# The tiled products of scores and values between the two products of the inverses' blocks

## The chip, the cores and the metric

One Trainium2 chip, one core. The metric is the device time of one execution in microseconds, the median over several runs. The kernel is written in Bass and Tile: Tile orders the instructions of each engine by priority and sets the semaphores; where the kernel asks for it, the order of TensorE's instructions is that of the program text.

## The reference

A trunk of one layer: 512 positions, width 2048, in two groups of channels, the first of 16 heads of 64 channels with a generalized delta rule, the second a multi-scale pooling. What matters here is the first:

```
def step(S, inp):
    r_t, w_t, k_t, v_t, kk_t, a_t = inp
    sa = jnp.einsum('bhvk,bhk->bhv', S, -kk_t)
    S = (S * w_t[:, :, None, :]
         + sa[..., None] * (kk_t * a_t)[:, :, None, :]
         + v_t[..., None] * k_t[:, :, None, :])
    y_t = jnp.einsum('bhvk,bhk->bhv', S, r_t)
    return S, y_t
```

Ahead of it stand an RMS norm, the projection `h @ w_in` to 6272 columns and a token shift; behind it a norm per head, a gate, the projections `w_out` and `w_pg`, an embedding term and a last RMS norm.

## The kernel before

**The stages.** First the input is normed, transposed and split into two parts (`hhi`, `hlo`); a dense product in this kernel is three matmuls of 128x128 on 512 columns (`mm3`, L164: high by high, high by low, low by high). Then, from about 55 to 715 us, eight pairs of heads `j` are worked off, two heads and 128 channels each, the 512 positions in 8 chunks of 64. The last stage is the two large projections with `w_out` and `w_pg`.

**The stream.** The recurrence over the chunks is a chain of small steps on TensorE, ScalarE and VectorE. So that TensorE does not idle meanwhile, the projections of the next pairs (`zr`, `zk`, `zv`, `zg`) and of the pooling group (`zb`, with `pp`) run between its steps: `stream()` (L461) is a generator that yields after every three dense matmuls, and `pump(n)` (L492) takes some n matmuls from it. It carries over what it took too much (`debt`). The weights of the stream come by DMA on SP's queue and are split by a cast on ScalarE (L132, `whi`) and a subtraction on VectorE (L133, `wlo`), two chunks ahead of their use.

**The order on TensorE.** From L345 on, `pin` is set: `mm` and `tr` (L156, L160) call `keep_in_program_order`, so TensorE runs its instructions in the order in which the code writes them. The other engines are ordered by Tile's priorities. `tc.high_priority(offset=HP)`, with HP = 1000, puts the instructions of its block ahead of others that could go as well.

**One pair.** `prepare(j)` scales keys and receptances; `scores(j)` (L608) makes the scores within chunks (`mt`, 64x64 blocks) and sends their 32x32 corners by DMA to a layout in which `invert(j)` (L650) inverts the unit triangular matrices on VectorE; the inverses' diagonal blocks come back by DMA into `x1`. `gather(j)` (L678) then finishes what the recurrence needs, and `recur(j)` (L756) runs it.

**`gather`, step by step, on TensorE** (every small product is in fp32, which TensorE runs as two matmul instructions; 16 products are 32 instructions):

- `decay_and_rate` for the next pair (`pu`, `pa`), transposes of the values (`pv`, L688) and of the keys (`pbk`, L699). ScalarE copies them to `uv` (L690, L691) and `bkn` (L700).
- `pump(H4)`: 8 dense matmuls, in effect 9.
- `pmv` (L704): 16 products of scores and values on 64x64 tiles. ScalarE copies the result into `zsp[0]` (L712) and `mv` (L713).
- `norm_key(j + 1)`: two dense matmuls `pss`, read by VectorE (L568).
- `pump(H5)`, the four transposes `pyt` of the pair before, `pump(HX)`.
- `pq` (L738): 16 products of 32x32 blocks, the scores' corner times the inverse's first block, which VectorE has transposed (`y1`, L734). ScalarE copies the result to `q2t` in two halves (L745; the profile calls the tile `q`).
- `pump(H1)`: 6 dense matmuls.
- `px` (L747): 16 products of 32x32 blocks, `q2t` times the inverse's second block. ScalarE copies the result into the corner of `x1` (L752; the profile calls the tile `x`).
- `pump(H1)`: 6 dense matmuls; then the recurrence begins with `pu`, which reads `x1` and `zsp[0]` (L793). `mv` is first read one step later, in the sum into `zs` (L787).

`pmv`, `pss`, `pyt`, `pq` and `px`, and ahead of them `pu`, `pa` and `pbk`, are tiles of the PSUM pool `psM` under one tag with three buffers; a fourth tile waits until the first one has been read.

Of the kernel before, what the change touches and what calls it, by code (L numbers as in the profile page):

```python
# [9 lines left out]
F32 = mybir.dt.float32  # L10
# [5 lines left out]
P = 128  # L16
# [7 lines left out]
C = 64  # L24
# [10 lines left out]
def trunk_kernel(ctx: ExitStack, tc: tile.TileContext, x, p, norm_g, w_in, mu, w0, w_up, a0, a_up,  # L35
                 k_k, k_a, r_k, ln_w, ln_b, w_pool, pool_scale, w_out, w_ple, w_pg, b_pg, final_g, out):
    nc = tc.nc
    PSUM = bass.MemoryType.PSUM
    x, p, w_in, w_out, w_ple, w_pg = x[0], p[0, 0], w_in[0], w_out[0], w_ple[0], w_pg[0]
# [8 lines left out]
    psM = s2.enter_context(tc.tile_pool(name="psM", bufs=3, space=PSUM))  # L48
# [107 lines left out]
    def mm(*a, **k):  # L156
        i = nc.tensor.matmul(*a, **k)  # L157
        return tc.keep_in_program_order(i) if pin[0] else i

    def tr(*a):  # L160
        i = nc.tensor.transpose(*a)
        return tc.keep_in_program_order(i) if pin[0] else i
# [178 lines left out]
    rw = s2a.enter_context(tc.tile_pool(name="rw", bufs=1))  # L341
# [18 lines left out]
    zsp = [rw.tile([P, P], F32, name=f"zs{i}") for i in range(2)]  # L360
# [131 lines left out]
    def pump(n):  # L492
        debt[0] += n
        while debt[0] > 0:
            c = next(big, None)
            if c is None:
                debt[0] = 0
                return
            debt[0] -= c
# [17 lines left out]
    H1, H2, H3, H4, H5, HE = 6, 12, 20, 8, 13, 40  # L517

    def decay_and_rate(j):

        (ur, us), (ar_, as_) = wab.pop(j)
        for raw, st, z_, lo, hi in ((ur, us, uaz[0], slice(64, 128), slice(0, 64)),
                                    (ar_, as_, uaz[1], slice(0, 64), slice(64, 128))):
            nc.scalar.copy(st, raw)
            nc.scalar.copy(z_[hi, :], raw[hi, :])
            nc.vector.tensor_tensor(st[lo, :], raw[lo, :], st[lo, :].bitcast(F32), ALU.subtract)

        ps = psM.tile([P, T], F32, name=f"pu{j}", tag="m")
        mm(ps, us, uhh, start=True, stop=False)
        mm(ps, uaz[0], lal, start=False, stop=True)  # L530
        sig = rw.tile([P, T], F32, name=f"sig{j}", tag="t", bufs=4)
        nc.scalar.activation(sig, ps, AF.Tanh, scale=0.5, bias=dp(81, j))
        nc.vector.tensor_scalar(sig, sig, 0.5, 0.5, ALU.mult, ALU.add)
        nc.vector.tensor_tensor_scan(sig, seg, sig, 0.0, ALU.mult, ALU.add)
        pw = rw.tile([P, NCH, C + 1], F32, name=f"pw{j}", tag="pw", bufs=2)
        ipw = rw.tile([P, NCH, C], F32, name=f"ipw{j}", tag="ipw")
        nc.gpsimd.memset(pw[:, :, 0:1], 1.0)
        sig3 = sig.rearrange("p (c t) -> p c t", t=C)
        nc.scalar.activation(pw[:, :, 1:C + 1], sig3, AF.Exp, scale=-KAPPA)
        nc.scalar.activation(ipw, sig3, AF.Exp, scale=KAPPA)  # L540


        ps = psM.tile([P, T], F32, name=f"pa{j}", tag="m")
        mm(ps, as_, ahh, start=True, stop=False)
        mm(ps, uaz[1], lal, start=False, stop=True)
        tha = rw.tile([P, T], F32, name=f"tha{j}", tag="tha")
        nc.scalar.activation(tha, ps, AF.Tanh, scale=0.5, bias=dp(25, j))
        pws[j] = (pw, ipw, tha)
# [5 lines left out]
    def prepare_key(j):  # L554
        k_ = need("k", j)
        kk = rw.tile([P, T], F32, name=f"kk{j}", tag="kk")
        nc.scalar.activation(kk, k_, AF.Square, scale=pc("k_k", j))
        kqh = rw.tile([P, T], F32R, name=f"kqh{j}", tag="t", bufs=4)
        kql = rw.tile([P, T], F32R, name=f"kql{j}", tag="t", bufs=4)
        split(kqh, kql, kk)  # L560
        kks[j] = (kk, kqh, kql)

    def norm_key(j):
        kk, kqh, kql = kks[j]
        ps = psM.tile([P, T], F32, name=f"pss{j}", tag="m")
        mm(ps, blk, kqh, start=True, stop=False)
        mm(ps, blk, kql, start=False, stop=True)
        late[0] = nc.vector.tensor_scalar(kk, ps, 1e-24, None, ALU.max)  # L568

    def scale_key(j):  # L570
        k_, kk = need("k", j), kks[j][0]
        nc.vector.reciprocal(kk, kk)
        nc.vector.scalar_tensor_tensor(kk, k_, pc("k_k", j), kk, ALU.mult, ALU.mult)
        kks[j] = kk
# [103 lines left out]
    def gather(j):  # L678
        d = st_[j]
        bk, v_, mt = d.pop("bk"), d.pop("v_"), d["mt"]  # L680
        if j + 1 < NJ:
            prepare_key(j + 1)
            decay_and_rate(j + 1)

        uv = rw.tile([P, NCH, P], F32, name=f"uv{j}", tag="uv")
        ps = psY.tile([P, T], F32, name=f"pv{j}", tag="y")
        for tt in range(NT):
            tr(ps[:, tt * P:(tt + 1) * P], v_[:, tt * P:(tt + 1) * P], ident)  # L688
        pv = ps.rearrange("p (t c) -> p t c", c=P)
        nc.scalar.copy(uv[0:64, 0::2, :], pv[0:64])  # L690
        nc.scalar.copy(uv[64:128, 1::2, :], pv[64:128])  # L691


        bkn = rw.tile([P, NCH, P], F32, name=f"bkn{j}", tag="bkn")
        for hf in range(2):
            ps = psM.tile([P, T], F32, name=f"pbk{j}_{hf}", tag="m")
            for i in range(4):
                ch = 4 * hf + i
                tr(ps[:, i * P:(i + 1) * P], bk[:, ch // 2, 2 * (ch % 2):2 * (ch % 2) + 2, :], ident)  # L699
            nc.scalar.copy(bkn[:, 4 * hf:4 * hf + 4, :], ps.rearrange("p (c n) -> p c n", n=P))  # L700

        pump(H4)

        ps = psM.tile([P, 8, C], F32, name=f"pmv{j}", tag="m")  # L704
        for u in range(8):
            for par in range(2):
                pb, kb = 64 * (1 - par), 64 * par
                h = u % 2
                mm(ps[pb:pb + 64, u, :], mt[kb:kb + 64, par, u, 1 - par, :],
                   uv[kb:kb + 64, 2 * (u // 2) + par, 64 * h:64 * h + 64], start=True, stop=True)  # L710
        mv = rw.tile([P, 4, P], F32, name=f"mv{j}", tag="mv")
        nc.scalar.copy(zsp[0][64:128, :].rearrange("p (h t) -> p h t", h=2), ps[64:128, 0:2, :])  # L712
        nc.scalar.copy(mv.rearrange("p q (h t) -> p (q h) t", h=2), ps)  # L713

        d.update(uv=uv, bkn=bkn, mv=mv)
        if j + 1 < NJ:
            norm_key(j + 1)
        pump(H5)
        if pending:
            pending.pop()()  # L720
        pump(HX)

        x1 = d["x1"]

        def units(fn):
            for u in range(8):
                for par in range(2):
                    fn(u, par, 64 * (1 - par))

        y1 = rw.tile([P, 8, 32], F32, name=f"y1{j}", tag="tm")  # L730

        with tc.issue_after(late[0].ins):
            for pb in (0, 64):
                yt = nc.vector.transpose(y1[pb:pb + 32], x1[pb:pb + 32, :, 0:32])  # L734
        if j + 1 < NJ:
            with tc.issue_after(yt.ins):
                scale_key(j + 1)
        ps3 = psM.tile([P, 8, 32], F32, name=f"pq2{j}", tag="m")  # L738
        units(lambda u, par, pb: mm(ps3[pb + 32:pb + 64, u, :],
                                                  mt[pb:pb + 32, par, u, 1 - par, 32:64],  # L740
                                                  y1[pb:pb + 32, u, :], start=True, stop=True,
                                                  tile_position=(pb, pb + 32)))
        q2t = rw.tile([P, 8, 32], F32, name=f"q2{j}", tag="xw")
        for pb in (0, 64):
            nc.scalar.copy(q2t[pb + 32:pb + 64], ps3[pb + 32:pb + 64])  # L745
        pump(H1)
        ps4 = psM.tile([P, 8, 32], F32, name=f"px2{j}", tag="m")  # L747
        units(lambda u, par, pb: mm(ps4[pb:pb + 32, u, :], q2t[pb + 32:pb + 64, u, :],
                                                  x1[pb + 32:pb + 64, u, 32:64], start=True, stop=True,
                                                  tile_position=(pb + 32, pb)))  # L750
        for pb in (0, 64):
            nc.scalar.copy(x1[pb:pb + 32, :, 32:64], ps4[pb:pb + 32])  # L752
        pump(H1)


    def recur(j, work, between):  # L756
# [115 lines left out]
    HP = 1000  # L872
# [11 lines left out]
    for _ in invert(0):  # L884
        pass
    pump(HT)
    gather(0)
    for j in range(NJ):
        def between():
# [291 lines left out]
```

## Time and profile before

| what | value |
|---|---|
| time, median of 3 runs | 1099.41 us (1097.35, 1099.41, 1099.85) |
| span of the profiled execution | 1095.9 us |
| median of the runs less that span | 3.5 us |
| stretch from 100 to 715 us: TensorE, VectorE, ScalarE busy | 611.5, 471.1, 262.7 of 615.0 us |

The span goes from the first to the last instruction of one profiled execution; the time of a run also holds what lies around it. The time of the profiled execution itself, apart from its span, is not listed, so the median of the runs stands beside it. A row of a timeline gives the start, the duration, the engine, the line, the operation, the tile written and the tiles read, the size of the part of the array that is used (rows\*columns), and how often; L157 is the line of the helper `mm`, so TensorE's rows are told apart by their tiles. The duration of a matmul covers its whole way through the array: the next one starts well before it ends, so starts are what to compare.

### The profile page before, as it was taken

The numbers are of one execution on the slowest core, as the hardware profiler recorded it, in microseconds if no ns is written. First come the engines' busy times: TensorE is split into PE (matmuls) and PEld (weight loads), VectorE is DVE, ScalarE is ACT, GpSimd is POOL, SyncE is SP. The second block draws the span as 40 slices with busy tenths as digits, with TensorE's granted clock in tenths as the row PEclk, the third lists the DMA queues.
The fourth block names the chain that finished last, engine by engine and source line by source line (L and its number), as shares of the span: only waits on it lengthen the run. The fifth ranks groups of instructions, "written<-read, shape, count | busy, mean of one in ns | idle before, by whom it ended". The sixth has DMA issues, their size and how long they took to land.

```text
span 1095.9 us, 17196 instructions
## 1 busy us (share of the span) xinstructions
PE 1070.8 (98%) x6060; PEld 877.6 (80%) x6060; DVE 708.2 (65%) x1835; ACT 448.3 (41%) x917; POOL 76.9 (7%) x180
## 2 busy tenths in 40 slices
PE   5999999999999999999999999999999999999996
PEld 4888878887788888788878788888888888888885
DVE  6687867878688679678886956454433424445366
ACT  7633535345335335353343344543222222233337
POOL 2100110110110110100101101000000000000000
PEclk9999999999999999999999999999999999999999
DMA  7433433332423333333334242775534438455534
GB/s 233 116 96 97 111 92 84 96 100 73 120 82 105 104 92 89 96 82 93 91 94 119 79 138 93 232 233 169 172 124 136 167 99 244 137 189 137 181 106 154
DMA packets 178486, 138.56 MB, mean 126 GB/s; under 512 B 34678, under 2 KB 139743, under 8 KB 178399
## 3 DMA queue, kind: packets, MB, share of 16 engines
q1 hardware_dynamic: 157694, 103.89, 32.1%
q10 hardware_dynamic: 20704, 33.56, 9.8%
q8 instruction: 48, 0.79, 0.3%
q14 instruction: 40, 0.32, 0.1%
HBM read 118.02 MB, written 18.87 MB: 125 GB/s over the span
## 4 chain that ended last, share of the span: by engine, by line
PE 86%; DVE 5%; DMA 4%; ACT 3%; issue 1%; SPq 0%; ACTq 0%; DVEq 0%
PE acc_o L157 16%; PE zb L157 14%; PE acc_g L157 14%; PE zv L157 8%; PE zk L157 7%; PE zg L157 7%; PE zr L157 7%; PE py L157 2%; PE pple L157 2%; PE pm L157 1%; PE pu L157 1%; DMA n<-nd 1%; PE pp L157 1%; DMA raw_g<-in_w_pg_dram 1%; PE ps L157 1%
## 5 line engine op out<-in xcount | busy, mean ns | idle before, releaser
L133 DVE TENSOR_TENSOR wlo_g<-raw_g,whi_g 128x512 fp32r<-128x512 f32 x84 | 57.0, 685 | 79.6 <-ACT whi_g L132 76.5
L157 PE MATMUL zb<-hhi,whi_b 128*128 128x512 f32 x256 | 107.0, 418 | 0.0
L133 DVE TENSOR_TENSOR wlo_o<-raw_o,whi_o 128x512 fp32r<-128x512 f32 x64 | 43.9, 690 | 91.4 <-ACT whi_o L132 91.4
L157 PE MATMUL zb<-hhi,wlo_b 128*128 128x512 f32 x256 | 100.5, 393 | 0.0
L157 PE MATMUL acc_o<-whi_o,ylo 128*128 128x512 f32 x256 | 100.2, 391 | 0.0
L157 PE MATMUL acc_o<-whi_o,yhi 128*128 128x512 f32 x256 | 99.9, 390 | 0.0
L157 PE MATMUL zb<-hlo,whi_b 128*128 128x512 f32 x256 | 99.9, 390 | 0.0
L157 PE MATMUL acc_o<-wlo_o,yhi 128*128 128x512 f32 x256 | 99.8, 390 | 0.0
L132 ACT CAST whi_g<-raw_g 128x512 fp32r<-128x512 f32 x84 | 51.9, 620 | 102.7 <-PE acc_g L157 55.4
L157 PE MATMUL acc_g<-whi_g,x2hi 128*128 128x512 f32 x208 | 81.3, 391 | 0.0
L157 PE MATMUL acc_g<-wlo_g,x2hi 128*128 128x512 f32 x208 | 80.9, 389 | 0.0
L157 PE MATMUL acc_g<-whi_g,x2lo 128*128 128x512 f32 x208 | 80.7, 389 | 0.0
L132 ACT CAST whi_o<-raw_o 128x512 fp32r<-128x512 f32 x64 | 39.9, 623 | 97.0 <-PE acc_o L157 96.7
L816 POOL TENSOR_SCALAR s0p<-sbd,pw 64x64 f32<-64x64 f32 x96 | 56.6, 589 | 322.8 <-DVE sbd L809 255.0
L132 ACT CAST whi_b<-raw_b 128x512 fp32r<-128x512 f32 x64 | 39.7, 621 | 86.5 <-PE zv L157 35.4
L133 DVE TENSOR_TENSOR wlo_b<-raw_b,whi_b 128x512 fp32r<-128x512 f32 x64 | 43.8, 685 | 34.2 <-ACT whi_b L132 32.9
L157 PEld LDWEIGHTS zb<-hhi,wlo_b 128*128 128x128 f32 x256 | 48.0, 188 | 11.1
L661 DVE TENSOR_TENSOR xw<-xw,tm 128x60 f32<-128x60 f32 (+24 forms) x248 | 52.1, 210 | 6.8
L157 PEld LDWEIGHTS acc_o<-wlo_o,yhi 128*128 128x128 f32 x256 | 48.1, 188 | 10.3 <-DVE wlo_o L133 0.4
L157 PEld LDWEIGHTS acc_o<-whi_o,yhi 128*128 128x128 f32 x256 | 48.1, 188 | 9.7
L157 PEld LDWEIGHTS acc_o<-whi_o,ylo 128*128 128x128 f32 x256 | 48.1, 188 | 9.8
L157 PEld LDWEIGHTS zb<-hhi,whi_b 128*128 128x128 f32 x256 | 48.2, 188 | 8.5
(285 smaller groups left out, 2550.0 us busy)
## 6 DMA issues: line engine op xcount, KB each, us to landing
raw_b<-in_w_in_dram SPq DMA_DIRECT2D x64, 256.0 KB
raw_o<-in_w_out_dram SPq DMA_DIRECT2D x64, 256.0 KB
raw_g<-in_w_pg_dram SPq DMA_DIRECT2D x64, 256.0 KB
raw_k<-in_w_in_dram SPq DMA_DIRECT2D x32, 256.0 KB
raw_r<-in_w_in_dram SPq DMA_DIRECT2D x32, 256.0 KB
raw_v<-in_w_in_dram SPq DMA_DIRECT2D x32, 256.0 KB
raw_g<-in_w_in_dram SPq DMA_DIRECT2D x32, 256.0 KB
n<-nd SPq DMA_DIRECT2D x16, 256.0 KB
```

What stands on the lines that cost most here:

```text
L132: nc.scalar.copy(hi, raw)
L133: nc.vector.tensor_tensor(lo, raw, hi.bitcast(F32), ALU.subtract)
L157: i = nc.tensor.matmul(*a, **k)
L661: nc.vector.tensor_tensor(xw[:, 0:n_, s + 1:32], xw[:, 0:n_, s + 1:32], tm[:, 0:n_, 0:w_], ALU.add)
L816: nc.gpsimd.tensor_scalar(s0p[hc, :], nxt[hc, hc], pcn[hc], None, ALU.mult)
```

## The change

The 16 products of scores and values (`pmv`, now written to `psv`, the same tile name in the profile) leave their place ahead of `norm_key` and stand between `pq` and `px`. The portion of 6 dense matmuls that stood between `pq` and `px` joins the portion behind `px`: 12 dense matmuls there. The copies into `zsp[0]` and `mv` come behind the copies into `x1`. The copies into `q2t` are given high priority. The order of the 16 products (by `u`, then `par`) and their operands stay as they were.

```
-        ps = psM.tile([P, 8, C], F32, name=f"pmv{j}", tag="m")
-        for u in range(8):
-            for par in range(2):
-                pb, kb = 64 * (1 - par), 64 * par
-                h = u % 2
-                mm(ps[pb:pb + 64, u, :], mt[kb:kb + 64, par, u, 1 - par, :],
-                   uv[kb:kb + 64, 2 * (u // 2) + par, 64 * h:64 * h + 64], start=True, stop=True)
-        mv = rw.tile([P, 4, P], F32, name=f"mv{j}", tag="mv")
-        nc.scalar.copy(zsp[0][64:128, :].rearrange("p (h t) -> p h t", h=2), ps[64:128, 0:2, :])
-        nc.scalar.copy(mv.rearrange("p q (h t) -> p (q h) t", h=2), ps)
-
-        d.update(uv=uv, bkn=bkn, mv=mv)
+        d.update(uv=uv, bkn=bkn)
         if j + 1 < NJ:
             norm_key(j + 1)
         pump(H5)
...
         q2t = rw.tile([P, 8, 32], F32, name=f"q2{j}", tag="xw")
-        for pb in (0, 64):
-            nc.scalar.copy(q2t[pb + 32:pb + 64], ps3[pb + 32:pb + 64])
-        pump(H1)
+        with tc.high_priority(offset=HP):
+            for pb in (0, 64):
+                nc.scalar.copy(q2t[pb + 32:pb + 64], ps3[pb + 32:pb + 64])
+        psv = psM.tile([P, 8, C], F32, name=f"pmv{j}", tag="m")
+        units(lambda u, par, pb: mm(psv[pb:pb + 64, u, :], mt[64 - pb:128 - pb, par, u, 1 - par, :],
+                                    uv[64 - pb:128 - pb, 2 * (u // 2) + par, 64 * (u % 2):64 * (u % 2) + 64],
+                                    start=True, stop=True))
         ps4 = psM.tile([P, 8, 32], F32, name=f"px2{j}", tag="m")
...
         for pb in (0, 64):
             nc.scalar.copy(x1[pb:pb + 32, :, 32:64], ps4[pb:pb + 32])
-        pump(H1)
+        mv = rw.tile([P, 4, P], F32, name=f"mv{j}", tag="mv")
+        nc.scalar.copy(zsp[0][64:128, :].rearrange("p (h t) -> p h t", h=2), psv[64:128, 0:2, :])
+        nc.scalar.copy(mv.rearrange("p q (h t) -> p (q h) t", h=2), psv)
+        d["mv"] = mv
+        pump(2 * H1)
```

## The prediction, made before the changed kernel was run

> **What bounds the kernel now.** I read the page first, then the table of who waited for whom, then the timeline of TensorE at the places that the change touches.
>
> ```profile
> span 1095.9 us, 17196 instructions
> PE 1070.8 (98%) x6060; PEld 877.6 (80%) x6060; DVE 708.2 (65%) x1835; ACT 448.3 (41%) x917; POOL 76.9 (7%) x180
> ...
> PE 86%; DVE 5%; DMA 4%; ACT 3%; issue 1%; SPq 0%; ACTq 0%; DVEq 0%
> ```
>
> TensorE is busy 98% of the span, and 86% of the chain that ended last lies on it. "Busy" is modelled from the ends of pipelined matmuls, so I looked for real waits:
>
> ```profile
> PE py L157 <- DVE sbd L809: 1.6, 4, 0.9
> PE pss L157 <- ACT bkn L700: 0.9, 2, 0.5
> ```
>
> Within the eight head pairs TensorE hardly waits for another engine; these are the two largest such waits, with the total, the count and the longest. One, `pss` for ScalarE's `bkn` copy, stands right behind the products that move. Everything else that can be won here is how TensorE's own instructions follow each other. The timeline of gather 0, with the start and the duration of each:
>
> ```profile
> 113.61 0.39 PE L157 MATMUL zv<-hhi,whi_v 128*128 128x512 f32 x1
> 113.84 0.39 PE L157 MATMUL zv<-hlo,whi_v 128*128 128x512 f32 x1
> 114.06 0.39 PE L157 MATMUL zv<-hhi,wlo_v 128*128 128x512 f32 x1
> 114.38 1.15 PE L157 MATMUL pmv<-uv,mt 64*64 64x64 f32 x32
> 115.46 0.50 PE L157 MATMUL pss<-kqh,blk 128*128 128x512 f32 x1
> 115.80 0.39 PE L157 MATMUL pss<-kql,blk 128*128 128x512 f32 x1
> ...
> 121.94 0.39 PE L157 MATMUL zb<-hhi,wlo_b 128*128 128x512 f32 x1
> 122.26 0.69 PE L157 MATMUL pq<-y,mt 32*32 32x32 f32 x32
> 122.89 0.50 PE L157 MATMUL zb<-hhi,whi_b 128*128 128x512 f32 x1
> 123.22 0.40 PE L157 MATMUL zb<-hlo,whi_b 128*128 128x512 f32 x1
> ...
> 124.15 0.39 PE L157 MATMUL zb<-hhi,wlo_b 128*128 128x512 f32 x1
> 124.47 0.69 PE L157 MATMUL px<-x,q 32*32 32x32 f32 x32
> 125.09 0.50 PE L157 MATMUL zb<-hhi,whi_b 128*128 128x512 f32 x1
> 125.43 0.40 PE L157 MATMUL zb<-hlo,whi_b 128*128 128x512 f32 x1
> ```
>
> Dense matmuls start 0.23 apart (113.61, 113.84, 114.06). A visit to small tiles breaks that pace three times: the first small product starts 0.32 after the last dense one, not 0.23; the first dense one starts 0.13 to 0.15 after the last small one; and the second dense one 0.33 or 0.34 after the first. I cost a visit from the last dense start to the second dense start behind it, less two paces (0.46): `pmv` 115.80 - 114.06 - 0.46 = 1.28 us, `pq` 123.22 - 121.94 - 0.46 = 0.82, `px` 125.43 - 124.15 - 0.46 = 0.82. That is 2.92 us per gather. The last of the eight gathers shows the same `pq` visit (648.67 + 0.34 - 647.73 = 1.28 again):
>
> ```profile
> 647.73 0.39 PE L157 MATMUL zb<-hhi,wlo_b 128*128 128x512 f32 x1
> 648.05 0.69 PE L157 MATMUL pq<-y,mt 32*32 32x32 f32 x32
> 648.67 0.50 PE L157 MATMUL zb<-hhi,whi_b 128*128 128x512 f32 x1
> 649.01 0.40 PE L157 MATMUL zb<-hlo,whi_b 128*128 128x512 f32 x1
> ```
>
> The group rows over all eight give what one small product takes, to find the start of the last one:
>
> ```profile
> L157 PE MATMUL pmv<-uv,mt x256: 218/218/267, 114.4 to 641.1; 64*64 64x64 f32 x128
> L157 PE MATMUL pq<-y,mt x256: 191/191/212, 122.3 to 648.5; 32*32 32x32 f32 x128
> ```
>
> So from the first start to the last, 32 products take 0.69 - 0.19 = 0.50 us on 32x32 tiles and 1.15 - 0.22 = 0.93 on 64x64; the wait from the last small start to the next dense one is 122.89 - 122.76 = 0.13 behind `pq` and 115.46 - 115.31 = 0.15 behind `pmv`.
>
> **Term 1: three visits become one.** No product is added or removed: the same 96 small products run, and the same dense ones (the two portions of 6 become one of 12, the next weights stand in the same order). Two entries and two exits to dense work go per gather; two changes of tile size come in, 32x32 to 64x64 and back. No row of this trace has such a change. Nearest are the entries and exits themselves. I take for each what the array leaves empty before the next tile shape may start, 0.13 behind 32x32 and 0.15 behind 64x64. One visit is then 0.32 + 0.50 + 0.13 + 0.93 + 0.15 + 0.50 + 0.13 + 0.33 - 0.46 = 2.53 us, against 2.92: 0.39 saved, eight times, 3.1 us. Bounds: if an inner change costs as much as going out to dense work and back, nothing is saved (0); if it costs only the pace of the small products (0.50/31 = 0.02 and 0.93/31 = 0.03), `px` would follow the last `pq` by 0.02 + 0.93 + 0.03 = 0.98 us instead of 1.21, and then the copy below sets it. The 0.32 in front of `pq` and the 0.13 behind it are the rows that decide for the middle.
>
> [...]
>
> **Term 2: the copy of `q`.** It loses its cover. `px` needs both halves of `q`, which ScalarE copies from `pq`. So far six dense matmuls ran in that time; now only `pmv` does.
>
> ```profile
> 123.05 0.74 ACT L745 COPY q<-pq 32x256 f32<-32x256 f32 x2 [1.74 <-issue]
> 123.81 0.62 ACT L132 CAST whi_g<-raw_g 128x512 fp32r<-128x512 f32 x1
> ```
>
> ```profile
>   PE pq L157: 9.9, 7
> ```
>
> The copies start 0.29 after the last `pq` (122.76) and end 1.03 after it. The row from the view of `q`'s tile counts why ScalarE stood idle before them: in 7 of 8 gathers it was waiting for `pq`, so nothing was ahead. The handover to TensorE is in these rows: `bkn` is two copies of 0.59, the first done at 189.27 + 0.59 = 189.86, and `pss` starts at 189.90, some 0.05 later.
>
> ```profile
> 189.27 1.07 ACT L700 COPY bkn<-pbk 128x512 f32<-128x512 f32 x2
> ...
> 189.90 0.50 PE L157 MATMUL pss<-kqh,blk 128*128 128x512 f32 x1 [0.45 <-ACT bkn L700]
> ```
>
> ```profile
> L700 ACT COPY bkn<-pbk x16: 566/588/597, 114.8 to 639.3; 128x512 f32<-128x512 f32 x16
> ```
>
> So `px` may start 1.03 + 0.05 = 1.08 us after the last `pq`, and by TensorE it would at 0.13 + 0.93 + 0.15 = 1.21. Hidden, with 0.13 to spare. The new high priority puts these copies ahead of other ready work, but not ahead of a cast already running. ScalarE is busy 41%, a cast runs 0.62, so an unlucky start adds up to 0.62 - 0.13; if busy 4 times in 10 with any rest of the cast equally likely, 0.4 x 0.49 x 0.49 / (2 x 0.62) = 0.08 per gather, 0.6 in all. Seven idle arrivals of eight speak for half of that: +0.3 us. If the inner changes were free, the floor of 1.08 would hold, so term 1 would win 0.13 x 8 = 1.0 more, not more.
>
> **Term 3: the stall of `pss`.** Three PSUM buffers rotate under one tag: `pa`, two of `pbk`, `pmv`, `pss`. `pss` is the third tile behind the first `pbk` and so waits for its `bkn` copy (0.9 us in two gathers). With `pmv` moved behind it, it takes the older buffer of `pa`, which `pmv` had entered with no wait. -0.9 us; at worst the delay shows up elsewhere (0).
>
> **What moves at no cost.** `zs` and `mv` are now copied after `x`:
>
> ```profile
> L712 ACT COPY zs<-pmv x8: 260/260/261, 116.6 to 641.3; 64x128 f32<-64x128 f32 x8
> L713 ACT COPY mv<-pmv x8: 586/587/587, 116.9 to 641.6; 128x512 f32<-128x512 f32 x8
> 125.64 0.74 ACT L752 COPY x<-px 32x256 f32<-32x256 f32 x2
> ```
>
> The recurrence's first product needs `x` and `zs`: 0.29 + 0.74 + 0.26 = 1.3 us behind the last `px`, under 12 dense matmuls (12 x 0.23 = 2.8). `mv` (0.59) is needed one hop later. Two casts of 0.62 fit in between; with three the product would wait. Behind these copies only casts are queued, whose weights are fetched two chunks ahead. `pq` needs VectorE's transposes `y`; these follow `pss`, which comes earlier with `pq` and keeps its distance to it. `psv` takes the buffer that `pss`'s reader on VectorE left. No moved step issues a DMA, and neither SP's nor POOL's queue is passed.
>
> **Sum.** -3.1 + 0.3 - 0.9 = -3.7 us, on the profiled span 1095.9 - 3.7 = 1092.2. The span lies 3.5 us below the median of the runs (1099.4), which holds what surrounds it; I keep that distance: 1095.7.
>
> **The rivals.** (a) Inner changes are free: -3.1 - 1.0 - 0.9, with the copies now on the path and 0.6 for casts: -4.4, 1095.0. For it: small products of one shape follow at 0.02. Against: the empty 0.13 to 0.15 at each exit. (b) Inner changes cost a full way out and back: only -0.9 + 0.3 remain, 1098.8. For it: no row shows them cheaper. (c) Slower: `px` stands right behind ScalarE's copies, and a cast of 0.62 and an activation of 0.60 (as L373's) run ahead of them in each gather. `q` comes 1.22 late, 1.09 is exposed, 8.7 in all: -3.1 - 0.9 + 8.7 = +4.7, 1104.1. It decides for slower from (4.0 + 2.2)/8 + 0.13 = 0.91 us of lateness per gather. Against: seven idle arrivals. (d) Given back: the recurrence's waits for VectorE (`sbd`) grow by as much as TensorE gains, 1099.4. For it: the first of the waits quoted above. Against: it is 1.6 us in all. (e) Issue: with no dense matmuls in which to queue them, 64 products come at the pace at which they are issued. If that were 0.06, as 32 `pm` products on 64x128 tiles go (2.06/32), `pmv` and `px` take 3.8 instead of 1.4: +2.4 per gather, 1115. Against: `pq`'s 32 start at 0.02, though perhaps from a backlog.
>
> ```profile
> 133.32 2.06 PE L157 MATMUL pm<-ar,bk 64*128 64x128 f32 x32
> ```
>
> [...]
>
> **The numbers.** About 0.2%, 2.2 us, can be told from no change (runs lay from 1097.4 to 1099.9). Forecast 0.57, (a) 0.10, (b) 0.14, (c) 0.09, (d) 0.07, (e) 0.03. Of the forecast's share 0.02 fall within 0.2%. Faster 0.55 + 0.10 = 0.65; same 0.02 + 0.14 + 0.07 = 0.23; slower 0.12. The range goes from the lower bound of the sum (-3.1 - 1.0 - 0.9 = -5.0, 1094.4, less 0.8, the mean distance of the three runs from their median) to (b) and most of (d): 1093.6 to 1099.2; it leaves out (c) and (e).
>
> **What would show it.** Term 1: in each gather `pq`, `pmv`, `px` in a row with gaps of 0.13 and 0.15, and 2.99 us from the last dense start before to the second behind. Term 2: `q` ends before `pmv` does, and no wait of `px` for L745 in the table. Term 3: the row `pss` for `bkn` gone. Wrong if `px` waits for `q` more than 0.4 us in most gathers, if small products start slower than 0.02 and 0.03 apart, or if `py` waits more for VectorE than the 1.6 us of now.

## The result and the profile after

The changed kernel takes 1095.35 us (median of 7 runs, 1093.32 to 1096.83) against 1099.41 for the kernel before beside it: a ratio of 0.9964, with a 95% interval of 0.9952 to 0.9976. That is 4 us faster, clear of the 0.2% below which nothing can be told. The forecast was 1095.7 us, and 1092.2 for the profiled span.

The page of the profile after shows the span, the busy times and the chain that ended last.

```profile
span 1092.3 us, 17194 instructions
PE 1067.4 (98%) x6060; PEld 879.1 (80%) x6060; DVE 707.9 (65%) x1835; ACT 448.2 (41%) x917; POOL 74.4 (7%) x180
...
PE 88%; DVE 5%; DMA 3%; ACT 2%; issue 1%; SPq 0%; ACTq 0%; DVEq 0%
```

As many matmuls as before, VectorE and ScalarE as busy as before; TensorE's busy time became 3.4 us shorter. The timeline of TensorE in gather 0 answers to the one of before:

```profile
114.01 0.39 PE L157 MATMUL zv<-hhi,wlo_v 128*128 128x512 f32 x1
114.24 0.39 PE L157 MATMUL pss<-kqh,blk 128*128 128x512 f32 x1
114.47 0.39 PE L157 MATMUL pss<-kql,blk 128*128 128x512 f32 x1
...
120.59 0.39 PE L157 MATMUL zb<-hhi,wlo_b 128*128 128x512 f32 x1
120.90 0.69 PE L157 MATMUL pq<-y,mt 32*32 32x32 f32 x32
121.53 1.15 PE L157 MATMUL pmv<-uv,mt 64*64 64x64 f32 x32
122.61 0.69 PE L157 MATMUL px<-x,q 32*32 32x32 f32 x32
123.23 0.50 PE L157 MATMUL zb<-hhi,whi_b 128*128 128x512 f32 x1
123.57 0.39 PE L157 MATMUL zb<-hlo,whi_b 128*128 128x512 f32 x1
```

`pss` now runs at the pace of its dense neighbours (0.23). One visit holds all three groups of small products: 123.57 - 120.59 - 0.46 = 2.52 us, where the three visits of before took 2.92. `pmv` starts 121.53 - 121.40 = 0.13 behind the last `pq` (120.90 + 0.50), `px` 122.61 - 122.46 = 0.15 behind the last `pmv`. The other seven gathers show the same times within 0.01 us.

The table of waits of TensorE for the other engines, beside that of before:

```profile
PE py L157 <- DVE sbd L806: 1.9, 6, 0.6
PE pu L157 <- ACT x L745: 1.0, 1, 1.0
...
PE pu L157 <- DVE zs L784: 0.7, 2, 0.4
```

The row of `pss` waiting for `bkn` is gone, and no row says that `px` waits for `q`. A new row is there: `pu`, the first product of the recurrence, waits 1.0 us for the copies into `x1`, in one gather. ScalarE's timeline in that gather, number 5, and TensorE's, show what held them:

```profile
494.58 0.74 ACT L735 COPY q<-pq 32x256 f32<-32x256 f32 x2 [2.30 <-PE pq L157]
495.66 0.26 ACT L747 COPY zs<-pmv 64x128 f32<-64x128 f32 x1 [0.34 <-PE pmv L157]
495.94 0.59 ACT L748 COPY mv<-pmv 128x512 f32<-128x512 f32 x1
497.56 0.33 ACTq L863 DMA_DIRECT2D yd<-yo  x1
497.93 0.62 ACT L132 CAST whi_k<-raw_k 128x512 fp32r<-128x512 f32 x1 [1.40 <-DVE sw L420]
498.89 0.62 ACT L137 CAST dh<-u 128x512 fp32r<-128x512 f32 x1 [0.35 <-DVE u L421]
499.42 0.73 ACT L745 COPY x<-px 32x256 f32<-32x256 f32 x2
```

```profile
498.80 0.39 PE L157 MATMUL zg<-hhi,wlo_g 128*128 128x512 f32 x1
500.20 0.49 PE L157 MATMUL pu<-zs,x 128*128 128x128 f32 x2 [1.02 <-ACT x L745]
```

```profile
496.85 0.68 DVE L862 TENSOR_TENSOR yo<-yo,sg 128x512 f32<-128x512 f32 x1
```

Three things stand ahead of `x` in ScalarE's order, besides `zs` and `mv`: the issue of the DMA that stores `yo`, for which ScalarE idles from 496.53 until VectorE has finished `yo` at 496.85 + 0.68 = 497.53; a cast; and the cast `dh`, which waits for VectorE's `u`. (The row of the first cast names `sw` as what ended ScalarE's idling; the DMA issue, which is not counted as busy, stands between.) `px` itself had ended by 496.3. In gather 1 the same DMA issue delays `pu` by 0.12.

### The profile page after: what moved, and what is told of

Its sections match the earlier page's. It is cut to its first block, busy times and chain, and to the rows that moved or that the text cites. A ratio compares the mean times of both kernels' runs of the same rounds, so it can differ in the third digit from the quotient of the medians.

```text
span 1092.3 us, 17194 instructions
## 1 busy us (share of the span) xinstructions
PE 1067.4 (98%) x6060; PEld 879.1 (80%) x6060; DVE 707.9 (65%) x1835; ACT 448.2 (41%) x917; POOL 74.4 (7%) x180
## 4 chain that ended last, share of the span: by engine, by line
PE 88%; DVE 5%; DMA 3%; ACT 2%; issue 1%; SPq 0%; ACTq 0%; DVEq 0%
PE acc_o L157 16%; PE acc_g L157 16%; PE zb L157 15%; PE zv L157 8%; PE zr L157 7%; PE zg L157 7%; PE zk L157 6%; DMA n<-nd 2%; PE py L157 2%; PE pple L157 2%; PE pu L157 2%; PE pm L157 1%; PE pp L157 1%; PE ps L157 1%; PE pmv L157 1%
```

## The experiments

**The changed kernel without the priority of `q`.** The two copies lose their `with tc.high_priority(offset=HP):`.

> The changed kernel without the high priority of the copies into q2t. My theory (the gain is three visits to small tiles made one, and the stall of pss gone): the copies wait for pq in any case, so nothing changes, 1095.4 us, 0.996 of before; it also shows how far a second profile of the same work differs in its recurrence waits. Rival (the priority is what lets px follow without a wait): px waits for q by up to 0.5 us in each gather, 1099 us.

Ratio 0.9965 (0.9953 to 0.9978); the rival falls. The order of the instructions is the same on every engine with and without this priority: it does nothing here, since ScalarE waits for `pq` anyway. So this kernel stands for the changed one in what follows. Its span was 1094.8 against 1092.3, with `py` waiting for `sbd` 4.3 us in place of 1.9, one wait of 2.8 among them. So much can two profiles of the same instructions differ, and nearly all of it in the recurrence: from the first dense matmul behind `pbk` to `pu`, the eight gathers together take 120.63 us in one and 120.62 in the other.

**`x1` at high priority too.**

```
-        for pb in (0, 64):
-            nc.scalar.copy(x1[pb:pb + 32, :, 32:64], ps4[pb:pb + 32])
+        with tc.high_priority(offset=HP):
+            for pb in (0, 64):
+                nc.scalar.copy(x1[pb:pb + 32, :, 32:64], ps4[pb:pb + 32])
```

> The changed kernel with the copies into x1 at high priority too. In the profile after, pu waits for x 1.02 us in gather 5 and 0.12 in gather 1, behind a DMA issue and casts on ScalarE. Theory: this wait is a new cost of the change, which goes with the order on ScalarE: no wait of pu for x, 1.1 us less than the changed kernel, 1094.2. Rival (the copies are late because px's neighbours on ScalarE wait for VectorE, whatever the order): the wait stays, 1095.4.

Ratio 0.9958 (0.9942 to 0.9974). ScalarE in gather 5:

```profile
496.25 0.33 ACTq L864 DMA_DIRECT2D yd<-yo  x1
496.62 0.62 ACT L132 CAST whi_k<-raw_k 128x512 fp32r<-128x512 f32 x1 [1.40 <-DVE sw L420]
497.14 0.73 ACT L746 COPY x<-px 32x256 f32<-32x256 f32 x2
497.90 0.62 ACT L137 CAST dh<-u 128x512 fp32r<-128x512 f32 x1
```

`x` now goes ahead of `dh`, though still behind the DMA issue, and `pu` waits 0.05 us in place of 1.02. Measured in the same way, the eight gathers are 4.40 us shorter than before, against 3.15 in the changed kernel: the order on ScalarE was the cause of this wait. A new wait of `pm` for VectorE's `bk` (0.6 us) gives part of it back.

**Three visits again, in the new order.**

```
-        pump(HX)
+        pump(HX - H1)
...
+        pump(3)
         psv = psM.tile([P, 8, C], F32, name=f"pmv{j}", tag="m")
...
+        pump(3)
         ps4 = psM.tile([P, 8, 32], F32, name=f"px2{j}", tag="m")
```

> The order of the changed kernel, but three visits again: 3 dense matmuls between pq and pmv, 3 between pmv and px, 6 fewer in front of pq; 12 behind px as in the change. My theory: each gather pays 2.92 us for its visits instead of 2.53, 3.1 us more than the changed kernel, 1098.5 us; the stall of pss stays away. Rival (the gain comes from the new order of the PSUM buffers and of ScalarE's copies, not from the number of visits): 1095.4 as the changed kernel.

Ratio 0.9986 (0.9975 to 0.9996), against 0.9965 for the first experiment on the same chip: 0.0021, 2.3 us of the 3.1 expected. Its timeline of TensorE in gather 0:

```profile
120.00 0.39 PE L157 MATMUL zb<-hhi,wlo_b 128*128 128x512 f32 x1
120.32 0.69 PE L157 MATMUL pq<-y,mt 32*32 32x32 f32 x32
120.94 0.50 PE L157 MATMUL zb<-hhi,whi_b 128*128 128x512 f32 x1
121.28 0.40 PE L157 MATMUL zb<-hlo,whi_b 128*128 128x512 f32 x1
121.51 0.39 PE L157 MATMUL zb<-hhi,wlo_b 128*128 128x512 f32 x1
121.83 1.15 PE L157 MATMUL pmv<-uv,mt 64*64 64x64 f32 x32
122.91 0.50 PE L157 MATMUL zb<-hhi,whi_b 128*128 128x512 f32 x1
```

Each group pays its own 0.32 in and 0.34 behind again. `pss` does not wait here either. Why less than 3.1 came is in the profile too: the visits are 3.4 us longer in all than in the change, but `pu` waits only 0.34 us for `x`, against 1.14 there. The eight gathers are 2.6 us longer than in the change and 0.56 shorter than before. So the order alone brings the smaller part, and the number of visits the larger.

**`pmv` behind `pss`, all else as before.** In the kernel before, the products `pmv` and their copies go behind `norm_key(j + 1)`.

> The kernel before, with pmv and its two copies moved only to behind pss; all three visits stay apart. Theory: pss takes the buffer of pa and no longer waits for bkn; pmv, two dense matmuls later, may wait for bkn by at most 0.1 us in two gathers: 0.9 us less than before, 1098.5. Rival (the late bkn copy holds whoever needs the next buffer): pmv waits for bkn instead, 0.5 us in two gathers, and the time stays 1099.4.

Ratio 1.0018 (1.0007 to 1.0028): slower, beyond the rival too. The waits and gather 1 (the row of `pmv` is cut off by the end of the window, at 26 of its 32 instructions):

```profile
PE py L157 <- DVE sbd L810: 4.1, 6, 1.3
PE pmv L157 <- ACT bkn L700: 3.3, 4, 1.1
```

```profile
189.77 0.39 PE L157 MATMUL pss<-kql,blk 128*128 128x512 f32 x1
191.23 0.97 PE L157 MATMUL pmv<-uv,mt 64*64 64x64 f32 x26 [1.07 <-ACT bkn L700]
```

```profile
190.59 1.07 ACT L700 COPY bkn<-pbk 128x512 f32<-128x512 f32 x2
```

The first `bkn` copy ends at 190.59 + 0.59 = 191.18, and `pmv` starts 0.05 later. My 0.1 was wrong: before, `pss` came to this buffer after the whole of `pmv`, now `pmv` comes to it after two dense matmuls, so it meets the late copy earlier and in four gathers, not two. The rival's mechanism holds, at a higher price than it named: 3.3 us of waiting in place of 0.9. The change escapes because the next tile behind its `pss` is `pyt`, 12 dense matmuls later (in gather 0 it is `pq`, later still).

**`pmv` in front of `pq`.** The lines of `psv` stand ahead of `ps3`; nothing covers the copies of `q`.

> The changed kernel with pmv in front of pq instead of behind it: pmv, pq, px in one visit, with the same two entries and exits and one inner change less, but nothing between pq and px while ScalarE copies q. Theory (px may start 1.07 us after the last pq, and pmv hides that): px waits for q in all eight gathers, 1.07 us after the last pq; a visit takes 0.32 + 0.93 + 0.15 + 0.50 + 1.07 + 0.50 + 0.13 + 0.33 - 0.46 = 3.47 us instead of 2.53, 7.5 us more than the changed kernel, 0.35% slower than before. Rival (only the number of visits counts; the copies are quick enough): the same time as the changed kernel or 1 us less.

Ratio 1.0084 (1.0054 to 1.0114), worse than expected. TensorE in gather 4, and in two stretches the granted clock (the share of its full clock that TensorE was granted; the third column from the end):

```profile
425.51 0.69 PE L157 MATMUL pq<-y,mt 32*32 32x32 f32 x32
427.33 0.69 PE L157 MATMUL px<-x,q 32*32 32x32 f32 x32 [1.13 <-issue]
427.96 0.68 PE L157 MATMUL zg<-hhi,whi_g 128*128 128x512 f32 x1
428.43 0.63 PE L157 MATMUL zg<-hlo,whi_g 128*128 128x512 f32 x1
428.86 0.63 PE L157 MATMUL zg<-hhi,wlo_g 128*128 128x512 f32 x1
```

```profile
428.00:431.00 3.00, 3.00 (x9) 2.35 (x9) 3.00 (x9) 0.72 (x2) 0.40 (x1) 0.52 0.62 200
432.00:435.00 3.00, 3.00 (x17) 2.53 (x16) 2.30 (x5) 1.65 (x4) 0.00 (x0) 1.00 0.06 13
```

`px` comes 427.33 - 426.01 = 1.32 us after the last `pq`, not 1.07, because ScalarE copied `zs` and `mv` first. A visit took 1.20 us more than in the change, 9.6 in all. And behind it the dense matmuls go at 0.43 apart, not 0.23, with the granted clock at half for some 3.4 us (its mean over 428 to 432 is 0.57; (1 - 0.57) x 4 / 0.5 = 3.4, an estimate). That happened three times in this profile (also at 582, behind gather 6, where the mean over 580 to 586 is 0.72, and at 612, near the end of a wait of 2.8 us of `py`, where the mean over 612 to 616 is 0.57). Half the clock for 3.4 us is 1.7 us, an estimate too; gathers 4 and 6 came out 2.8 us longer than in the change, 1.6 beyond the 1.20. 9.6 + 3 x 1.6, less the 1.1 by which `pu` no longer waits, plus 2.4 by which `py` waits longer, are 15.7; the spans differ by 15.9.

**One more pair of changes inside the visit.** `units` takes a range of `u`, with two products for each, and the visit runs `pq` 0 to 3, `pmv` 0, `pq` 4 to 7, `pmv` 1 to 7, `px`.

> The changed kernel with one more pair of changes of the tile size inside the visit: half of pq, 2 of pmv's 16 products, the other half of pq, the other 14 of pmv, px. Theory (each change of the size costs what it takes for the last small product to leave the array, 0.13 behind 32x32 and 0.15 behind 64x64): 0.28 - 0.05 = 0.2 us more per gather, 1.8 us more than the changed kernel; 28 pmv instructions still cover the copies of q (0.13 + 0.84 + 0.15 = 1.12 over 1.07). Rival (inside a visit a change costs nothing, the saving is all in the first entry and the last exit): no difference beyond 0.2 us, and gaps of 0.02 to 0.03 in the trace.

Ratio 0.9985 (0.9975 to 0.9994) beside before, against 0.9965: 2.2 us for 1.8 expected. The 0.9965 is from another chip, though, and the same kernel gave 0.9977 later, which would leave 0.9 us. The times alone do not settle it; the rows do. Gather 1:

```profile
195.35 0.39 PE L157 MATMUL zb<-hhi,wlo_b 128*128 128x512 f32 x1
195.67 0.44 PE L157 MATMUL pq<-y,mt 32*32 32x32 f32 x16
196.04 0.33 PE L157 MATMUL pmv<-uv,mt 64*64 64x64 f32 x4
196.30 0.44 PE L157 MATMUL pq<-y,mt 32*32 32x32 f32 x16
196.67 1.03 PE L157 MATMUL pmv<-uv,mt 64*64 64x64 f32 x28
197.63 0.69 PE L157 MATMUL px<-x,q 32*32 32x32 f32 x32
198.25 0.50 PE L157 MATMUL zb<-hhi,whi_b 128*128 128x512 f32 x1
198.59 0.40 PE L157 MATMUL zb<-hlo,whi_b 128*128 128x512 f32 x1
```

The visit is 198.59 - 195.35 = 3.24 us against 2.98, 0.26 longer (0.30 in gathers 0 and 7, where `px` waits a little for `q`). Each change takes the 0.12 to 0.15 again, wherever it stands (`pmv` 196.04 behind the last `pq` at 195.67 + 0.44 - 0.19 = 195.92).

**`pmv` in front, but `q` copied first.** As the fifth, with `zs` and `mv` under `tc.issue_after` of the last `q` copy.

> pmv in front of pq as in the fifth experiment, but the copies of zs and mv held behind those of q. There they ran first and px came 1.32 us after the last pq instead of 1.07, and in that profile the granted clock fell to 0.5 for 3.4 us three times, twice behind such a wait. Theory (copy chain of 0.24 + 0.74 + 0.05 to 0.1): px 1.03 to 1.1 us after the last pq, 0.2 us less per gather, 2 us less than that experiment; if the shorter wait also keeps the clock up, 5 us more: 1102 to 1106. Rival (the handover to TensorE, not the order of the copies, made the 0.25): px again 1.3 us behind, the same time as the fifth, 1108.

Ratio 1.0031 (1.0019 to 1.0044), 1100.4 us. Gather 1, TensorE and ScalarE:

```profile
197.51 0.69 PE L157 MATMUL pq<-y,mt 32*32 32x32 f32 x32
199.09 0.69 PE L157 MATMUL px<-x,q 32*32 32x32 f32 x32 [0.89 <-issue]
```

```profile
198.25 0.74 ACT L739 COPY q<-pq 32x256 f32<-32x256 f32 x2 [3.38 <-PE pq L157]
199.01 0.26 ACT L748 COPY zs<-pmv 64x128 f32<-64x128 f32 x1
```

`px` starts 199.09 - 198.01 = 1.08 us after the last `pq`: the prediction's floor (1.12 in gathers 0 and 7). The granted clock stayed full until the kernel's end: of the page's 40 slices of the span only the last has less than 0.9, and the mean is 0.997. The rival falls: the 0.25 of the fifth experiment were the order of the copies. By the ratios this is 5.8 us less than the fifth, within the 2 to 7 expected; the time itself lies below the expected 1102 to 1106.

**Both versions once more, on one chip.** The change with `x1` at high priority, and the one without priorities.

> The second experiment's kernel (the change with the copies into x1 at high priority) once more, beside the changed kernel on the same chip. Theory: the wait of pu for x is gone in this profile too, 1.1 us less than the changed kernel in the next column. Rival: the gain in the gathers is given back in the recurrence, and the times agree within 0.3 us.

> The first experiment's kernel once more: the changed kernel in all but the priority of q, with the same order of instructions on every engine. It stands for the changed kernel beside the run before. Both theories: 0.9965 of before, within 0.001.

Ratios 0.9960 (0.9944 to 0.9976) and 0.9977 (0.9966 to 0.9988); medians 1093.0 and 1094.9. The second is 0.0012 from the expected 0.9965, a little outside the 0.001. The wait of `pu` for `x` is 0.05 us in the first and 1.1 in the second, and the eight gathers take 119.38 and 120.63 us, as in the earlier profiles of each order (119.38, and 120.63 and 120.62). With the earlier pair (0.9958 and 0.9965) the kernel with `x1` at high priority was ahead by 0.7 and 1.7 thousandths. It has the lowest ratios of the study, though the intervals overlap, so its time is not shown to be better; the shorter gathers are.

## Why the prediction was right

**Term 1, one visit for three (-3.1).** 2.52 us a gather, 2.53 foreseen. Splitting the visit lost 2.3 us, and one more pair of changes made it 0.26 us longer in each gather. That an inner change costs the same 0.12 to 0.15 us as a way out to dense work, and neither nothing nor a way out and back, was the choice on which the term hung, and the third and sixth experiments show both ends wrong (rivals (a) and (b)). The time alone would not have told: 1095.35 lies as near to the 1095.0 of (a) as to the forecast; the rows decide.

**Term 2, the copy of `q` (+0.3).** Nothing in this profile. The floor of 1.08 and the 0.13 of cover were right, as the seventh experiment shows (1.08 in six gathers, 1.12 in two); that a cast would be running when `pq` ends did not come true in any gather, in this profile or in the two others of the same order. Without the cover the copy costs 7 us or more (`px` waited 7.2 us in the seventh experiment and 9.1 in the fifth): rival (c) had the mechanism, but no reason here to set in.

**Term 3, the stall of `pss` (-0.9).** Gone, as foreseen: no row of `pss` for `bkn`. The reason given, which buffer comes next, was half of it: the other half is how long after `bkn` the next tile is wanted, as the fourth experiment shows.

**What moves at no cost.** This step failed, by 1.1 us. I counted the casts that could fit ahead of `x1`, two of them. What came was an instruction that waits: a DMA issue on ScalarE's queue, standing still for VectorE (in gather 5 ScalarE idled from 496.53 to 497.56), with the copies queued behind it. That "only casts are queued" there was wrong; so was the order, for ScalarE ran `zs` and `mv` ahead of `x` in all eight gathers. The wait shows in all three profiles of this order and all but goes when `x1` gets the priority (0.05 us is left).

**Rivals (d) and (e).** One of the prediction's own signs against it came up: `py` waits more for VectorE than the 1.6 us of before. The waits for `sbd` are 1.9, 4.3 and 3.5 us in three profiles of one order; a part of the gain may go there, as (d) has it, and with one profile of before the runs do not settle how much. Not all of it went there. For (e), 32 small products still start within 0.50 and 0.93 us with nothing dense between, 0.02 and 0.03 apart and not the rival's 0.06.

**The sum.** The gathers became 3.15 us shorter in the profile; the errors of terms 2 (-0.3) and of the copies (+1.1) partly cancel. That the span was met within 0.1 us is luck: the same order gave 1092.3, 1094.8 and 1093.7. So is the step from span to median, the 3.5 us that I kept: in every run of the changed kernel, the time is 1.7 to 1.8 us above the span of the same execution, and the rest (about 1.7 before, 1.3 after) is that both profiled executions were quicker than the median. The measured ratios, 0.9964, 0.9965 and 0.9977, are what the -3.7 us (0.9966) is to be held against.

## What to carry to other kernels

Count how often TensorE goes from one tile shape to another, and cost each crossing from starts in the timeline; putting small products of different sizes next to each other paid here, 2.52 us a gather in place of 2.92, with the copy between them covered, and 0.13 us of cover was enough. When work is moved, look at the moved copies' neighbours in their engine's order for instructions that wait, a DMA issue above all, not only at how long they run. Where a dense stream is broken by a microsecond of idling, look at the granted clock as well: in the fifth experiment it took 1.6 us on top of the 1.20, in the two gathers where it fell.

## What the runs showed of the hardware

The granted clock fell to half for about 3.4 us behind waits of 1.13 us in a visit of 4.2 us (two of eight gathers of the fifth experiment), and never behind waits of 0.89 to 0.93 us in a visit of 3.9 to 4.0 (the seventh). All four runs of the fifth had a mean granted clock of 0.990 to 0.996, all ten of the seventh 0.997 or 0.998. Waits of 1.07 and 1.08 us ahead of `pmv` in the fourth, between dense matmuls and one visit, left the clock full (0.998 in the mean of that execution). A wait of 2.8 us in the recurrence ended in half the clock once (the fifth: 0.57 over 612 to 616) and once not (the first: 0.998 in the mean). What decides between one case and the next is not settled by these runs.
